# A diffusion layer from the output product on: weights as the moving operand, tokens standing, and the residual kept as rows

## The chip, the cores and the metric

The kernel runs on one core of a Trainium2 chip. The metric is the time of one execution on the device, in microseconds (us). The core has a matrix engine (PE, which multiplies a moving operand of up to 512 columns by a standing one of 128 x 128), a vector engine (DVE), a scalar engine (ACT), a general engine (POOL), and a queue that only issues transfers (SP). PE writes to PSUM, eight banks of 512 float32 columns; DVE and ACT read from it.

## The reference

One layer of a hybrid backbone on 1280 tokens of width 1024: 1024 latent tokens (eight blocks of 128) and 256 prompt tokens (two blocks), with a conditioning vector each.

```python
h = rms_norm(x, norm_mix_w) * (1.0 + sc1) + sh1
z = h @ w_in                        # recurrence q, f, f, i, g; attention q, k, v; gates gl
o_a = block_attention(q, k_all, v_all)
o_h = hgrn_branch(...)              # two directions, 4 heads, f = lb + (1 - lb) * sigmoid(hf), key = 1 - f
merged = g[:, :, 0] * (o_h @ w_ho) + g[:, :, 1] * (o_a @ w_ao)
x = x + g1 * (merged @ w_out)
h = rms_norm(x, norm_ffn_w) * (1.0 + sc2) + sh2
x = x + g2 * (jnp.square(jax.nn.relu(h @ w_ff1)) @ w_ff2)
y = rms_norm(x, final_norm_w)
```

All of it is float32. g1 and g2 are vectors of 1024 for each of the two conditions, latent and prompt.

## The kernel before

**Products.** Each float32 factor is split into a rounded high part (ACT, the first line of `split`) and the rest (DVE, its second line), and a product is three matmuls: high by high, high by rest, rest by high. Tokens come in three tiles `TT`: t=0 and t=1 with 512 latents each, t=2 with the 256 prompt tokens.

**Order of the work.** Projections and attention come first, then the recurrence, with the gate columns of w_in (and the conditioning product) filling PE between its small matmuls: a `Filler` deals them out in portions. Then come the branch products with the merge, the output product, the up-projection (w_ff1), and the down-projection (w_ff2). PE follows the order of the program. ACT, DVE, POOL and SP are ordered by a scheduler that simulates the program, with priority by program order; `tc.high_priority` moves an instruction ahead. From the up-projection on, SP too follows the order of the program. Each engine works strictly in its order.

**PSUM.** Three rings of banks: g (3), s (3) and t (2). Name p stands for g.

**Recurrence.** 24 units (`HUnit`: head, direction, tile). `prep` loads f and q, makes products of f along time by two scans on DVE, then k = 1 - f on ACT (in place of f), the scaled keys and queries on POOL and DVE. `keys_t` transposes keys to a bank of t, which ACT copies (`ukt`). `scores` makes scores in a bank of s, which DVE masks (`usm`); `states_` makes the states (s). `out`, one unit later, makes the outputs in a bank of g, which is copied on ACT (forward) or added to the forward output on DVE (`uo`, backward). The gate columns use banks of g.

**Output product.** The result has columns of w_out on partitions and tokens along the free axis: 128 x 128 pieces of w_out stand, the merged columns `mT` move (512 or 256 tokens). 48 groups (4 column pairs, 3 tiles, 2 halves), 24 matmuls each. `x_cols` loads x by columns (24 loads) and transposes it on PE; the group's sum is scaled by g1, which is a scalar for each partition here, and added in one DVE operation; `sq_acc` sums squares on ACT and DVE. `norm2_rstd` and `norm2` make the norm's factor by matmuls with a column of ones, spread it over partitions by matmuls with the identity, and apply it on DVE and ACT. `keep` stores the residual: latents as columns (`XA`), the prompt transposed to rows (`XT`).

**Up-projection.** The prompt's part is 32 groups of 24 matmuls of 256 columns. The latents' part uses Strassen's scheme with seven products: `sums1` builds the sums of activation blocks between the prompt's groups and `fsplit` splits them (`form`: B11 to T4). `fsums` does the same for weights.

**Down-projection.** Seven chains of 16 steps (`chain2`: P1, P2, P6, P7, P4, P5, P3) into five banks, 15 matmuls of 512 columns a step. For the latents (banks 0 to 3) weights `wh` stand and activations `ah` move; for the prompt's quarter (bank 4, `mm_p`) activations stand and weights move. `load_step` loads three steps ahead. `drain` adds finished banks to the residual, `gadd` in one DVE operation for latents, `pmul` and `padd` in two for the prompt. `sk` keeps P1's banks as a share of three other quarters, added later by `rest`. `final` transposes a block of latent columns to rows (8 transposes), and applies the last norm.

## Time and profile before

| | |
|---|---|
| runs | 2142.56, 2142.61, 2151.43 us; median 2142.61 |
| profiled execution | 2138.14 us; span 2136.4 us |
| mean granted PE clock | 0.993 |
| bytes moved | 316.64 MB in 251465 packets, mean 148 GB/s |

The profile shows one execution. Its page has busy times of the engines, and the groups of instructions with how long the engine stood idle before them and what ended that. "PE ps_g L302" is a matmul of line 302 into a bank of ring g, "A <- B" means that A waited until B was done. PEld is the loading of the standing operand, which goes on beside matmuls. Matmuls are pipelined: a record's duration is longer than the distance from one start to the next. In a table by windows a granted clock of 1.00 is full speed.

### The profile page before, as it was taken

The page shows a single profiled execution, that of the slowest core. Times are in us where ns is not written, and L with a number is a line of the kernel's source. Part 1 is how long each engine was busy: PE and PEld are TensorE (multiplying, and loading weights), DVE is VectorE, ACT ScalarE, POOL GpSimd, SP SyncE. Part 2 cuts the span into 40 slices and gives each one's busy share as a digit, 9 for nine tenths or more (in the row PEclk, how much of TensorE's full clock was granted, in tenths as well). Part 3 has the DMA queues.
Part 4 walks back from the last instruction along what each step waited for, and adds up shares of the span by engine and source line. Part 5 has one row for each costly group of instructions (what it writes and reads, how often), then busy time and mean ns, then how long its engine had stood idle before and what let it go on. Part 6 is the DMA issues. An engine that isn't in the chain of part 4 may idle for free.

```text
span 2136.4 us, 34621 instructions
## 1 busy us (share of the span) xinstructions
PE 2066.4 (97%) x12859; PEld 1779.6 (83%) x12859; DVE 1386.3 (65%) x2620; ACT 970.9 (45%) x2003; POOL 514.5 (24%) x545
## 2 busy tenths in 40 slices
PE   6899999999999999998999999999999999999998
PEld 4788889988899987887888888898888888888876
DVE  3784776676776888777353525966666665566684
ACT  4754555555555522222230425754555444333352
POOL 1372323332332445444112100222211110000010
PEclk9999999999999999999999999999999999999999
DMA  9365221241222255454634433674444488565763
GB/s 287 111 188 163 65 75 37 75 132 54 69 80 70 85 172 161 145 161 136 210 119 138 127 103 111 215 229 158 140 156 143 149 308 258 175 190 170 237 223 104
DMA packets 251465, 316.64 MB, mean 148 GB/s; under 512 B 18440, under 2 KB 171600, under 8 KB 251296
## 3 DMA queue, kind: packets, MB, share of 16 engines
q1 hardware_dynamic: 238912, 274.79, 40.8%
q0 software_dynamic: 12384, 39.64, 5.2%
q8 instruction: 101, 1.65, 0.3%
q14 instruction: 68, 0.56, 0.1%
HBM read 226.81 MB, written 87.56 MB: 147 GB/s over the span
## 4 chain that ended last, share of the span: by engine, by line
PE 48%; issue 29%; DVE 9%; DMA 7%; POOL 4%; ACT 3%; SPq 1%; POOLq 0%; DVEq 0%; ACTq 0%
PE ps_g L302 8%; PE ps_g L304 7%; PE ps_g L303 7%; PE ps_s L661 4%; PE ps_t L702 3%; POOL AF L102 3%; PE ps_g L718 2%; PE ps_g L717 2%; PE ps_g L318 2%; PE ps_g L320 2%; PE ps_g L319 2%; DMA wraw<-in_w_in 2%; PE ps_s L302 1%; PE ps_s L303 1%; PE ps_s L304 1%
## 5 line engine op out<-in xcount | busy, mean ns | idle before, releaser
L302 PE MATMUL ps_g<-hs,wsp 128*128 128x512 f32 (+1 forms) x960 | 357.8, 373 | 7.5 <-DVE uo L952 7.2
L304 PE MATMUL ps_g<-hs,wsp 128*128 128x512 f32 (+1 forms) x960 | 342.7, 357 | 0.0
L303 PE MATMUL ps_g<-hs,wsp 128*128 128x512 f32 (+1 forms) x960 | 342.1, 356 | 0.0
L680 POOL TENSOR_SCALAR pexp<-pexp,rs 128x512 f32<-128x512 f32 (+1 forms) x104 | 169.7, 1638 | 366.2 <-ACT pTh L705 184.2
L273 ACT ACTIVATE wsp<-wraw 128x1024 fp32r<-128x1024 f32 x118 | 117.9, 1000 | 260.8 <-PE ps_g L303 109.6
L274 DVE TENSOR_TENSOR wsp<-wraw,wsp 128x1024 fp32r<-128x1024 f32 x118 | 139.2, 1180 | 121.4 <-ACT wsp L273 121.0
L302 PEld LDWEIGHTS ps_g<-hs,wsp 128*128 128x128 f32 x960 | 182.3, 190 | 33.0 <-DVE uo L952 7.7
L304 PEld LDWEIGHTS ps_g<-hs,wsp 128*128 128x128 f32 x960 | 181.9, 190 | 27.3
L303 PEld LDWEIGHTS ps_g<-hs,wsp 128*128 128x128 f32 x960 | 182.7, 190 | 19.8
L705 ACT ACTIVATE pTh<-ps_t 128x512 fp32r<-128x512 f32 x200 | 118.9, 601 | 124.7 <-PE ps_t L702 122.2
L273 ACT ACTIVATE ah<-ar 128x640 fp32r<-128x640 f32 (+1 forms) x112 | 81.0, 723 | 199.1 <-PE ps_g L1479 185.6
L662 DVE TENSOR_REDUCE mx<-ps_s 128x1 f32<-128x512 f32 (+1 forms) x208 | 136.6, 662 | 51.3 <-PE ps_s L661 50.9
L672 ACT ACTIVATE pexp<-ps_s,ngm 128x512 f32<-128x512 f32 (+1 forms) x208 | 137.3, 669 | 43.1 <-DVE ngm L666 41.5
L706 DVE TENSOR_TENSOR pTl<-ps_t,pTh 128x512 fp32r<-128x512 f32 x200 | 135.8, 680 | 15.7 <-ACT pTh L705 15.2
L274 DVE TENSOR_TENSOR ah<-ar,ah 128x640 fp32r<-128x640 f32 (+1 forms) x112 | 89.8, 802 | 75.6 <-ACT ah L273 74.8
L661 PE MATMUL ps_s<-Kl,Ql 128*128 128x512 f32 (+1 forms) x416 | 128.0, 413 | 1.1 <-ACT pexp L672 1.1
L702 PE MATMUL ps_t<-ident,pexp 128*128 128x128 f32 x800 | 120.7, 273 | 3.0 <-DVE pTl L706 1.8
L318 PE MATMUL ps_g<-wsp,hs 128*128 128x256 f32 x400 | 117.4, 293 | 0.0
L319 PE MATMUL ps_g<-wsp,hs 128*128 128x256 f32 x400 | 114.0, 285 | 2.8 <-DVE wsp L274 2.8
L320 PE MATMUL ps_g<-wsp,hs 128*128 128x256 f32 x400 | 114.1, 285 | 0.0
L718 PE MATMUL ps_g<-pTl,Vl 128*128 128x256 f32 x400 | 106.1, 287 | 4.2 <-DVE pTl L706 4.1
L717 PE MATMUL ps_g<-pTh,Vl 128*128 128x256 f32 x400 | 105.9, 285 | 1.3 <-DVE oa L727 1.0
(389 smaller groups left out, 5368.0 us busy)
## 6 DMA issues: line engine op xcount, KB each, us to landing
ar<-AF SPq DMA_DIRECT2D x112, 320.0 KB, 3.2
wraw<-in_w_ff SPq DMA_DIRECT2D x32, 1024.0 KB, 6.0
wr<-in_w_ff SPq DMA_DIRECT2D x128, 256.0 KB, 3.7
wraw<-in_w_in SPq DMA_DIRECT2D x19, 1024.0 KB, 5.7
wraw<-in_w_ada SPq DMA_DIRECT2D x16, 1024.0 KB, 5.5
AF<-a POOLq DMA_DIRECT2D x48, 256.0 KB, 2.8
AF<-t POOLq DMA_DIRECT2D x48, 256.0 KB, 2.6
wa<-in_w_ada SPq DMA_DIRECT2D x32, 256.0 KB, 5.6
```

What stands on the lines that cost most here:

```text
L273: s_.activation(hi, raw, AF.Copy)
L274: v.tensor_tensor(lo, raw, f32(hi), op=ALU.subtract)
L302: pe.matmul(out, hi[:, k, :], mh, start=(first and k == 0), stop=False)
L303: pe.matmul(out, hi[:, k, :], ml, start=False, stop=False)
L304: pe.matmul(out, lo[:, k, :], mh, start=False, stop=(last and k == kcs - 1))
L318: pe.matmul(po[:, bb, :], mh[:, off:off + P], wh[:, k % 4, :], start=(k == 0), stop=False)
L319: pe.matmul(po[:, bb, :], mh[:, off:off + P], wl[:, k % 4, :], start=False, stop=False)
L320: pe.matmul(po[:, bb, :], ml[:, off:off + P], wh[:, k % 4, :], start=False, stop=(k == KC - 1))
L661: pe.matmul(pq[:, 0:n], self.qh[:, q0:q0 + P], K[self.g][var][self.kts[i]], start=(var == 0), stop=(var == 1))
L680: NORM[(i + j) % len(NORM)].tensor_scalar(x, x, self.rs[j], None, op0=ALU.mult)
L702: pe.transpose(pt[:, a, j * P:(j + 1) * P], self.Ps[j][i][:, b * P:(b + 1) * P], ident)
L718: pe.matmul(pv[:, 0:256], V[self.g][kg][:, b, :], lo[:, a, :], start=False, stop=(k == last))
```

## The change

- **Recurrence.** k = 1 - f goes to POOL. The outputs use ring s. The copies `ukt`, `usm` and `uo` get high priority.
- **Order of tiles** in the merge: t = 0, 2, 1.
- **Output product.** Tokens on partitions, columns along the free axis: a 128 x 128 piece of `mT` stands, 512 columns of w_out move; ten blocks of 128 tokens by two halves, 24 matmuls each. All of w_out is split into `WO` ahead, its first half during the merge, its second after it. x is loaded as rows. The gates, now along the free axis, are written as rows once (`gate_rows`) and read back spread over partitions; the add is two DVE operations (`out_add`). Squares are summed by ACT's accumulator; `out_norm` scales the row and stores the residual (`X1`); `norm2_t` transposes the normalised rows to columns.
- **Up-projection.** The transposes of t=1 run in groups 2 to 5 of the prompt's part. Two of the seven forms, B22 and T4, are split after it. Buffers are laid out anew (`H`, `slot`).
- **Down-projection.** All five banks use `mm_p`, activations standing. Drains are `gmul` and `radd`. The rings of the three sets of banks differ (`five`). `final` works on rows without transposes.

The diff, cut to its core:

```diff
+    def H(t, dt=F32R, name="hs"):
+        return hp.tile([P, 512] if t < 2 else [P, 2, 256], dt, tag="h%d" % t, name=name, bufs=16 if t < 2 else 8)
...
             k = self.k = f
-            s_.activation(k[:, 0:n], f[:, 0:n], AF.Identity, scale=-1.0, bias=1.0)
+            g_.tensor_scalar(k[:, 0:n], f[:, 0:n], -1.0, 1.0, op0=ALU.mult, op1=ALU.add)
...
             self.kts = S((P, 4, P), name="ukt")
-            s_.activation(self.kts[:, 0:self.nb], kt[:, 0:self.nb], AF.Copy)
+            with tc.high_priority(offset=400):
+                s_.activation(self.kts[:, 0:self.nb], kt[:, 0:self.nb], AF.Copy)
...
             self.sm = S((P, 4, P), name="usm")
-            v.tensor_tensor(self.sm[:, 0:nb], sc[:, 0:nb], masks[d].unsqueeze(1).broadcast_to([P, nb, P]), op=ALU.mult)
+            with tc.high_priority(offset=400):
+                v.tensor_tensor(self.sm[:, 0:nb], sc[:, 0:nb], masks[d].unsqueeze(1).broadcast_to([P, nb, P]), op=ALU.mult)
...
-            po = PS("p", (P, 4, P))
+            po = PS("s", (P, 4, P))
...
             o = self.o = S((P, 4, P), name="uo")
-            v.tensor_tensor(o[:, 0:nb], po[:, 0:nb], fwd.o[:, 0:nb], op=ALU.add)
+            with tc.high_priority(offset=400):
+                v.tensor_tensor(o[:, 0:nb], po[:, 0:nb], fwd.o[:, 0:nb], op=ALU.add)
...
     for cond in range(2):
         v.scalar_tensor_tensor(s2[:, cond], modc[:, cond, 32:40], 1.0, cols[:, NFFN:NFFN + 8], op0=ALU.add, op1=ALU.mult)
-        v.tensor_scalar(g1h[:, cond], modc[:, cond, 16:24], 0.5, None, op0=ALU.mult)
+        v.tensor_scalar(gc[:, 8 * cond:8 * cond + 8], modc[:, cond, 16:24], 0.5, None, op0=ALU.mult)
+        v.tensor_copy(out=gc[:, 16 + 8 * cond:24 + 8 * cond], in_=modc[:, cond, 40:48])
+    def gate_rows():
+        pt = PS("t")
+        pe.transpose(pt[0:32, 0:P], gc, ident)
+        e = S((32, P), name="gt0")
+        s_.activation(e, pt[0:32, 0:P], AF.Copy)
+        store(GR, e)
+    def gate_row(i, cond):
+        r = 16 * i + 8 * cond
+        return GR[r:r + 8, :].rearrange("(o a) b -> o (a b)", o=1).broadcast_to([P, D])
+    MT = (0, 2, 1)
-    for t, (t0, n, cond) in enumerate(TT):
+    for t in MT:
+        n = TT[t][1]
...
+    WO = [[None] * 4 for _ in range(2)]
+    def out_raw(half, kh):
+        r = wp.tile([P, 4, 512], F32, tag="wraw", name="wraw", bufs=2)
+        dma(r, I["w_out"][kh * 512:kh * 512 + 512, half * 512:half * 512 + 512].rearrange("(k p) c -> p k c", p=P))
+        return r
+    def out_w(half, kp, raw):
+        n = 2 * (4 * half + kp)
+        WO[half][kp] = hi, lo = [wsp((P, 2, 512)) if j < 4 else
+                                 (wo1 if j < 11 else wo2).tile([P, 2, 512], F32R, tag="wo%d" % j, name="wo") for j in (n, n + 1)]
+        split(hi, lo, raw)
     for c2 in range(4):
-        raws = []
...
             oc = 2 * c2 + half
             wh, wl = w_oc(r, half)
-            for t, (t0, n, cond) in enumerate(TT):
+            if oc == 1:
+                gate_rows()
+            for t in MT:
+                n = TT[t][1]
...
+        if c2 == 3:
+            for kp in range(4):
+                if kp % 2 == 0:
+                    raw = out_raw(0, kp // 2)
+                out_w(0, kp, raw[:, 2 * (kp % 2):2 * (kp % 2) + 2, :])
-    for t, (t0, n, cond) in enumerate(TT):
+    for t in MT:
...
+    xa = [[None] * KC for _ in range(2)]
+    h2 = [None] * KC
+    def new_cols(t):
+        if t == 0:
+            for t, kc in [(t, kb) for kb in range(4) for t in range(2)] + [(t, kb + 4) for t in (1, 0) for kb in range(4)]:
+                xa[t][kc] = H(0, F32, "xa")
+        elif t == 2:
+            for kc in range(0, KC, 2):
+                hi, lo = H(2), H(2)
+                h2[kc], h2[kc + 1] = [(hi[:, j], lo[:, j]) for j in range(2)]
+    xrow = {}
+    def load_row(b):
+        xrow[b] = xn.tile([P, D], F32, tag="x1", name="x1", bufs=6)
+        dma(xrow[b], xrows(b))
+    def load_g1b(t):
+        g = ob.tile([P, D], F32, tag="g1b", name="g1b", bufs=1)
+        dma(g, gate_row(0, TT[t][2]))
+        return g
+    def out_add(b, half, po, ss):
+        c = slice(half * 512, half * 512 + 512)
+        x, y = xrow[b][:, c], ob.tile([P, 512], F32, tag="y1", name="y1", bufs=2)
+        v.tensor_tensor(y, po, g1b[:, c], op=ALU.mult)
+        v.tensor_tensor(x, x, y, op=ALU.add)
+        s_.activation(y, x, AF.Square, accum_out=ss[:, half:half + 1])
+    def out_norm(b, ss):
+        dma(X1[b], xrow[b])
+        rst = T(4, "nrst")
+        v.tensor_tensor(ss[:, 2:3], ss[:, 0:1], ss[:, 1:2], op=ALU.add)
+        rstd_of(rst[:, 0:1], ss[:, 2:3], 1, 1.0 / D)
+        v.tensor_scalar(xrow[b], xrow[b], rst[:, 0:1], None, op0=ALU.mult)
+    def norm2_t(t, kc):
+        nb, cond = NB[t], TT[t][2]
+        pt = PS("t", (P, 4, P))
+        for j in range(4):
+            kj, b = (kc, j) if t < 2 else (kc + j // 2, j % 2)
+            pe.transpose(pt[:, j, :], xrow[4 * t + b][:, kj * P:(kj + 1) * P], ident)
+        if t < 2:
+            s_.activation(xa[t][kc], pt.rearrange("p b c -> p (b c)"), AF.Identity, scale=s2[:, cond, kc:kc + 1],
+                          bias=modc[:, cond, 24 + kc:25 + kc])
-            norm2_rstd(0)
+        hx = ob.tile([P, 4, P], F32, tag="y1", name="hx", bufs=2)
+        for j in range(2):
+            s_.activation(hx[:, 2 * j:2 * j + 2], pt[:, 2 * j:2 * j + 2], AF.Identity, scale=s2[:, cond, kc + j:kc + j + 1],
+                          bias=modc[:, cond, 24 + kc + j:25 + kc + j])
+        for j in range(2):
+            hi, lo = h2[kc + j]
+            split(hi, lo, hx[:, 2 * j:2 * j + 2].rearrange("p b c -> p (b c)"))
+    OB = (0, 1, 2, 3, 8, 9, 4, 5, 6, 7)
+    load_row(OB[0])
+    load_row(OB[1])
+    for kp in range(4):
+        if kp % 2 == 0:
+            raw = out_raw(1, kp // 2)
+        out_w(1, kp, raw[:, 2 * (kp % 2):2 * (kp % 2) + 2, :])
+    todo2 = []
+    for i, b in enumerate(OB):
+        t, off = b // 4, (b % 4) * P
+        if b in (0, 8, 4):
+            g1b = load_g1b(t)
+        ss = T(4, "oss2")
+        for half in range(2):
+            po = PSG()
+            for k in range(KC):
+                mh, ml = (x[:, off:off + P] for x in mT[t][k])
+                wh, wl = (x[:, k % 2, :] for x in WO[half][k // 2])
+                pe.matmul(po, mh, wh, start=(k == 0), stop=False)
+                pe.matmul(po, mh, wl, start=False, stop=False)
+                pe.matmul(po, ml, wh, start=False, stop=(k == KC - 1))
+                if half and todo2:
+                    todo2.pop(0)()
+            out_add(b, half, po, ss)
+            if half == 0 and i + 2 < len(OB):
+                load_row(OB[i + 2])
+        out_norm(b, ss)
+        if b in (3, 9):
+            new_cols(t)
+            todo2 = [lambda t=t, kc=kc: norm2_t(t, kc) for kc in range(0, KC, 1 if t == 0 else 2)]
...
...
+    def slot(f):
+        if f == "B22":
+            return H(2).rearrange("p a c -> p (a c)")
+        return H(1 if f in ("B21", "T1") else 0)
-        hi, lo = form[f][kb]
-        if lo is None:
-            lo = form[f][kb][1] = xp.tile([P, 512], F32R, tag="xa", name="form", bufs=18)
-        split(hi, lo, src)
+        hl = form[f][kb]
+        for i in range(2):
+            if hl[i] is None:
+                hl[i] = slot(f)
+        split(*hl, src)
...
+            fsplit("B21", kb, b21)
             t1 = t1s[kb] = pw.tile([P, 512], F32, tag="t1", name="t1", bufs=2)
             v.tensor_tensor(t1, b12, b11, op=ALU.subtract)
-            fsplit("T1", kb, t1)
             fsplit("B11", kb, b11)
         elif part == 1:
-            t3 = pw.tile([P, 512], F32, tag="t1", name="t3", bufs=2)
+            t3 = t3s[kb] = pw.tile([P, 512], F32, tag="t1", name="t3", bufs=2)
             v.tensor_tensor(t3, b22, b12, op=ALU.subtract)
             v.tensor_tensor(b12, b22, t1s[kb], op=ALU.subtract)
-            fsplit("B21", kb, b21)
-            fsplit("T3", kb, t3)
+            fsplit("T1", kb, t1s[kb])
         else:
             v.tensor_tensor(b21, b21, b12, op=ALU.subtract)
-            fsplit("B22", kb, b22)
+            fsplit("T3", kb, t3s[kb])
             fsplit("T2", kb, b12)
-            fsplit("T4", kb, b21)
     for i in range(NP):
...
             wt = w_oc(r, half)
-            mid = {3: lambda: norm2_rstd(1), 4: lambda: norm2(1)}.get(j)
+            mid = (lambda: (norm2_t(1, 2 * j - 4), norm2_t(1, 2 * j - 3))) if 2 <= j < 6 else None
             po = PSG()
             mm3(po[:, 0:256], wt, KC, h2, mid=mid)
...
     w_next = fsums(raw1(0))
-    close("pw", "h2p")
+    close("pw", "xn")
+    for kb in range(4):
+        fsplit("B22", kb, xa[1][kb + 4])
+    for kb in range(4):
+        fsplit("T4", kb, xa[0][kb + 4])
...
-        return ev.tile([P, 512], F32, tag="ev", name=name, bufs=14)
+        return ev.tile([P, 512], F32, tag="ev", name=name, bufs=13)
...
+        if 20 <= n < 36 and n % 2 == 0:
+            load_x1(row_loads.pop(0))
         if n == 54:
             load_fw()
         if n in (12, 14):
-            dma(xt[n // 2 - 6], XT[n // 2 - 6])
+            load_x1(8 + n // 2 - 6)
+        if n in (16, 18):
+            dma(g2b[n // 2 - 8], gate_row(1, n // 2 - 8))
...
-            more = dict(skip_group_check=not first)
-            for m in range(4):
+            for m in range(4 if name == "P3" else 5):
                 c = slice(m * P, (m + 1) * P)
-                pe.matmul(banks[m], wh[:, c], ah[:, 0:512], start=first and i == 0, stop=False, **more)
-                pe.matmul(banks[m], wh[:, c], al[:, 0:512], start=False, stop=False, **more)
-                pe.matmul(banks[m], wl[:, c], ah[:, 0:512], start=False, stop=i == NP - 1, **more)
-            if name != "P3":
-                mm_p(banks[4], i, (ah[:, 512:640], al[:, 512:640]), (wh, wl), first, False)
+                mm_p(banks[m], i, (ah[:, c], al[:, c]), (wh, wl), first)
+    xt = [None] * 10
+    def load_x1(b):
+        xt[b] = xo.tile([P, D], F32, tag="x1", name="x1", bufs=10)
+        dma(xt[b], X1[b])
...
+    def gmul(half, m, src):
+        y = cs("y")
+        v.tensor_tensor(y, src, g2b[m // 4][:, half * 512:half * 512 + 512], op=ALU.mult)
         return y
-    def padd(b, i, y):
-        c = slice(i * 512, (i + 1) * 512)
-        v.tensor_tensor(xt[b][:, c], xt[b][:, c], y, op=ALU.add)
-    def drain(t, half, banks, b):
+    def radd(t, half, m, y):
+        x = xt[blk(t, m)][:, half * 512:half * 512 + 512]
+        v.tensor_tensor(x, x, y, op=ALU.add)
+    def drain(t, half, banks):
         with tc.high_priority(offset=400):
-            for m in range(4):
-                gadd(t, 4 * half + m, banks[m])
-            y = pmul(half, banks[4])
-        padd(b, half, y)
+            for m, po in enumerate(banks):
+                radd(t, half, m, gmul(half, m, po))
...
+    def final(b, put=store):
+        ss, rst = ssf[b], T(4, "frst")
+            x = xt[b][:, c]
+            v.scalar_tensor_tensor(x, x, rst[:, 0:1], fw[:, c], op0=ALU.mult, op1=ALU.mult)
+            put(out_rows(b)[:, c], x)
...
+    X = five("gggss")
     chain2("P1", X, True)
-    chain2("P2", X, False, {2: make_g2b})
-    drain(0, 0, X, 0)
-    Y = five()
+    chain2("P2", X, False)
+    drain(0, 0, X)
+    Y = five("ttsgg")
     chain2("P6", Y, True)
-    drain(1, 0, Y, 1)
-    rest = [lambda t=t, h=h, m=m: gadd(t, 4 * h + m, sk[m]) for t, h in ((0, 1), (1, 0), (1, 1)) for m in range(4)]
-    rest += [lambda b=b, h=h: padd(b, h, pmul(h, sk[4])) for b, h in ((0, 1), (1, 0), (1, 1))]
+    drain(1, 0, Y)
+    yk = {}
+    def share(m, j):
+        if j == 0:
+            yk[m] = gmul(1, m, sk[m])
+            radd(0, 1, m, yk[m])
+        elif j == 1:
+            radd(1, 1, m, yk[m])
+        else:
+            radd(1, 0, m, gmul(0, m, sk[m]))
+    rest = [lambda m=m, j=j: share(m, j) for m in range(5) for j in range(3)]
     chain2("P7", Y, False, dict(enumerate(rest[0:8], 4)))
-    drain(1, 1, Y, 1)
+    drain(1, 1, Y)
     chain2("P4", Y, False, dict(enumerate(rest[8:], 4)))
-    drain(0, 1, Y, 0)
-    Z = five()
-    at = {3 * b + 2: lambda b=b: final(0, b) for b in range(4)}
+    drain(0, 1, Y)
+    Z = five("gsstt")
+    at = {}
+    for j, b in enumerate((0, 1, 2, 3, 8)):
+        at[3 * j + 1] = lambda b=b: (square(b, 0), square(b, 1))
+        at[3 * j + 2] = lambda b=b: final(b)
     chain2("P5", Z, True, at)
-    drain(1, 1, Z, 1)
-    at = {3: lambda: square_p(0, 0), 4: lambda: square_p(0, 1), 6: lambda: final_p(0), 8: lambda: square_p(1, 1)}
-    chain2("P3", Z, False, at)
+    drain(1, 1, Z)
+    chain2("P3", Z, False, {2 * j + 4: lambda b=b: square(b, 1) for j, b in enumerate((4, 5, 6, 7, 9))})
     for m in range(4):
-        gadd(1, m, Z[m])
+        radd(1, 0, m, gmul(0, m, Z[m]))
+        square(4 + m, 0)
+    for m in range(4):
+        final(4 + m, dma)
     for i in range(NP):
-        mm_p(Z[4], i, p3f[i], p3w[i], False, True)
-        if i in (3, 6, 9, 12):
-            final(1, i // 3 - 1, "ts"[i // 3 % 2] * 2, dma)
-    padd(1, 0, pmul(0, Z[4]))
-    square_p(1, 0)
-    final_p(1, dma)
+        mm_p(Z[4], i, p3f[i], p3w[i], False)
+    radd(1, 0, 4, gmul(0, 4, Z[4]))
+    square(9, 0)
+    final(9, dma)
```

215 lines of the change are left out of this document (46 added, 169 removed).

## The prediction

> **What bounds the kernel now.** The page's first lines come first, then a table of the stages by windows of time.
>
> ```profile
> span 2136.4 us, 34621 instructions
> PE 2066.4 (97%) x12859; PEld 1779.6 (83%) x12859; DVE 1386.3 (65%) x2620; ACT 970.9 (45%) x2003; POOL 514.5 (24%) x545
> ```
>
> PE is busy for 97% of the span: a change pays if it takes matmuls away or ends one of PE's few stops, and work taken from another engine alone is worth nothing. The profiled execution took 2138.1 us, 1.7 more than its span and 4.5 less than the median of 2142.6; I sum against 2138.1 and add 4.5 at the end. The stages that the change touches are the recurrence, output product, up-projection (prompt part, then the latents' seven products), down-projection and end. The columns are the stretch, its length, then busy time and instructions of PE, weight loads, DVE, ACT and POOL, the granted clock, and DMA:
>
> ```profile
> 720.00:1040.00 320.00, 303.28 (x2504) 258.44 (x2503) 244.02 (x585) 97.91 (x260) 140.96 (x154) 0.97 0.47 149
> 1200.00:1322.00 122.00, 119.80 (x672) 103.15 (x670) 46.60 (x81) 37.61 (x70) 2.09 (x2) 1.00 0.33 108
> 1322.00:1424.00 102.00, 97.37 (x797) 95.20 (x796) 88.70 (x141) 77.59 (x142) 23.32 (x30) 1.00 0.72 223
> 1424.00:1735.00 311.00, 310.98 (x1351) 252.91 (x1349) 198.01 (x274) 152.98 (x228) 62.09 (x114) 1.00 0.46 155
> 1735.00:2112.00 377.00, 374.85 (x1663) 307.86 (x1664) 248.74 (x389) 150.66 (x265) 10.43 (x17) 1.00 0.66 213
> 2112.00:2136.40 24.40, 15.26 (x83) 12.43 (x81) 11.11 (x24) 5.79 (x18) 2.72 (x5) 0.88 0.28 108
> ```
>
> The recurrence is the one stage with much to win: PE stands for 320 - 303.3 = 16.7 us there, and it alone of the first five rows has a clock under 1.00. The up-projection's prompt part loses 4.6 us. The view of waits says for whom PE stood:
>
> ```profile
> PE ps_g L302 <- DVE uo L952: 7.2, 2, 4.9
> PE ps_s L921 <- ACT ukt L902: 3.2, 3, 1.4
> PE ps_t L900 <- DVE usf L871: 1.7, 1, 1.7
> PE ps_g L940 <- ACT ze L1011: 1.2, 1, 1.2
> PE ps_s L304 <- DVE wsp L274: 2.6, 4, 1.0
> PE ps_g L304 <- DVE wsp L274: 1.7, 1, 1.7
> PE ps_t L1119 <- ACT xte L1176: 1.5, 1, 1.5
> PE ps_t L1174 <- ACT xte L1176: 0.7, 1, 0.7
> ```
>
> The first four are the recurrence's, the next two the prompt part's, and the last two fall where the prompt's residual is turned to rows for keeping. The longest, 7.2 us, is a gate matmul that has no free bank of ring g because an output of the recurrence still lies in one, waiting for its add on DVE.
>
> **The change part by part: small matmuls.** What disappears on PE are transposes and one-column or broadcast matmuls: the final rows' (L1543), the kept prompt rows' (L1174), the second norm's sums and broadcasts (L1139, L1148) and the prompt gate's (L1565). A mean duration overlaps its neighbours, so I price by starts:
>
> ```profile
> L1543 PE MATMUL ps_t<-ident,xa 128*128 128x128 f32 x48 | 6.2, 272 | 0.0
> L1543 PE MATMUL ps_s<-ident,xa 128*128 128x128 f32 x16 | 2.1, 272 | 0.0
> L1148 PE MATMUL ps_t<-ident,nrst 128*128 128x128 f32 x20 | 2.8, 280 | 0.0
> L1139 PE MATMUL ps_t<-ones,qacc 128*128 128x1 f32 x20 | 2.4, 238 | 0.0
> L1174 PE MATMUL ps_t<-ident,xa 128*128 128x128 f32 x16 | 2.4, 281 | 0.7 <-ACT xte L1176 0.7
> L1565 PE MATMUL ps_t<-ident,modc 128*128 128x128 f32 x16 | 1.9, 275 | 0.0
> 2115.15 1.03 PE L1543 MATMUL ps_s<-ident,xa 128*128 128x128 f32 x8
> 2115.94 0.48 PE L1478 MATMUL ps_g<-p3w,p3f 128*128 128x512 f32 x1
> 2116.26 0.40 PE L1479 MATMUL ps_g<-p3w,p3f 128*128 128x512 f32 x1
> 1249.51 0.28 PE L302 MATMUL ps_g<-hs,wsp 128*128 128x256 f32 x1
> 1249.98 0.28 PE L303 MATMUL ps_g<-hs,wsp 128*128 128x256 f32 x1
> ```
>
> Eight transposes take 2115.94 - 2115.15 = 0.79 us, and the matmul behind them 0.32 us where its like takes 0.23 (311 us over 1351 in the latents' stretch), so 0.88 for eight, 0.11 each. The six rows count 48 + 16 + 20 + 20 + 16 + 16 = 136, which is **-15.0 us**, all on PE's path. The 80 transposes that bring x to columns (10 blocks by 8 pieces) stay 80: the new second norm needs as many, later. One is added, for the gate rows: 0.1.
>
> **The products.** The prompt's 192 matmuls of 256 columns in the output product become 96 of 512. Four of the narrow take 0.47 us (1249.98 - 1249.51), so 192 take 22.6 and 96 wide ones at 0.23 take 22.1: **-0.5**. In the down-projection each step keeps 15 matmuls of 512 columns; exchanging what stands costs nothing, because the prompt's columns already run with tokens standing:
>
> ```profile
> L1508 PE MATMUL ps_g<-ah,wh 128*128 128x512 f32 x192 | 75.2, 392 | 0.0
> L1478 PE MATMUL ps_g<-wh,ah 128*128 128x512 f32 x96 | 37.5, 391 | 0.2 <-DVE yp L1570 0.2
> ```
>
> **Stops in the middle.** Nothing is turned to rows for keeping, so the two waits for xte go: **-2.2**. In the prompt part DVE is busy for 88.7 of 102 us and loses the latents' second-norm scalings and eight form splits, 16 operations on whole tiles. Of its 4.3 us of waits for weight splits I take half, **-2.2**, between nothing and all.
>
> **The recurrence.** Its outputs leave ring g for ring s, and the copies that free banks go ahead in DVE's and ACT's order. What stands behind a stop is its clock; the same view in short stretches:
>
> ```profile
> 834.00:836.80 2.80, 0.57 (x24) 0.30 (x12) 2.08 (x6) 0.00 (x0) 1.11 (x1) 1.00 0.32 117
> 836.80:840.30 3.50, 3.43 (x35) 2.21 (x35) 2.65 (x8) 1.45 (x6) 0.81 (x2) 0.51 0.34 72
> 888.00:891.50 3.50, 2.07 (x13) 1.74 (x13) 2.38 (x5) 1.94 (x8) 1.55 (x2) 0.99 0.45 152
> 891.50:895.00 3.50, 3.50 (x12) 2.69 (x11) 3.50 (x6) 2.10 (x6) 1.53 (x1) 0.52 0.11 43
> 986.00:989.50 3.50, 3.50 (x8) 2.77 (x9) 2.77 (x10) 1.93 (x8) 0.81 (x2) 0.50 0.59 188
> ```
>
> After each stop PE runs about 3.5 us at half clock, which loses 1.75. The two stops for uo (7.2) lie before the first and third such stretch: with them go 3.5, together **-10.7**, which I take whole, because a gate tile then finds a third bank. The stops for ukt and ze (4.4) and the half clock at 891.5 (1.75) are ACT's; they are left out, since ACT's new order is nowhere shown: the range has them, 6.1 more. *TensorE: Matmul & The Clock Gate* of the Trainium skill (Part 1) says that the clock falls after an idle window of about 3.4 us; by that only the 4.9 us stop would return clock, and my time would be 1.75 us higher. The rows here decide otherwise: the clock fell behind a stretch in which PE still worked 2.07 of 3.5 us.
>
> Moving 1 - f to POOL frees ACT, which stands in order behind it, but puts a longer instruction on the way to the keys:
>
> ```profile
> L847 ACT ACTIVATE uf<-uf 128x512 f32<-128x512 f32 (+1 forms) x24 | 13.4, 560 | 76.1 <-DVE usf L844 40.5 <-DVE usf L840 28.8 <-DVE usf L839 3.8
> L680 POOL TENSOR_SCALAR pexp<-pexp,rs 128x512 f32<-128x512 f32 (+1 forms) x104 | 169.7, 1638 | 366.2 <-ACT pTh L705 184.2
> L871 DVE TENSOR_TENSOR uw<-uq,um x24: 410/896/1508, 743.5 to 1024.7; 128x512 f32<-128x512 f32 x16, 128x256 f32<-128x256 f32 x8
> L274 DVE TENSOR_TENSOR wsp<-wraw,wsp 128x1024 fp32r<-128x1024 f32 x118 | 139.2, 1180 | 121.4 <-ACT wsp L273 121.0
> 2127.84 0.68 DVE L1570 TENSOR_TENSOR yp<-ps_g,g2b 128x512 f32<-128x512 f32 x1
> 2129.09 0.68 DVE L1576 TENSOR_TENSOR xt<-xt,yp 128x512 f32<-128x512 f32 x1
> ```
>
> 1.64 for 0.56 is 1.08 us more per unit. POOL has 141 us of work in 320, so it is hidden but at the first unit, where PE already waited 1.7 us for usf: **+1.1**. Behind it on POOL wait the unit's own key product, the scaled queries and the score add of the unit before.
>
> **What is added.** (1) The second half of w_out is split only when the merged tiles leave room: at worst eight merged splits of 0.68 and four weight splits of 1.18 follow one another, 10.2 us, where PE asks for the first after 24 x 0.23 = 5.5: a stop of 4.7, with clock 6.4; at best all is early. I take **+1.0**, near the low end, because DVE is busy for only 46.6 of 122 us there. (2) A drain is now two DVE operations a bank (0.68 + 0.68) where PE fills a bank in 0.69. Three drains are followed by a product into the same banks: the fifth bank is read 5 x 1.36 - 0.68 = 6.1 us after the first is full, PE wants it after 8 x 0.69 = 5.5: 0.6 each, **+1.8**; nothing if the scheduler reads all banks first, 8.4 if a step's splits (2.2) stand ahead each time. The 15 shares skipped between are covered by 377 - 249 us of idle DVE. (3) At the end four blocks want 16 DVE operations while PE does 48 matmuls (11 us): 16 x 0.68 is 10.9, as long as PE's part, with three short steps for each block between, so **+1.0**, between 0 and 2. (4) Eight splits of B22 and T4 move into the first latent pair; DVE has 113 idle us in that stretch, cost 0; without that cover 8 x 0.68 = 5.4. (5) DMAs: 24 column loads, 20 stores and 18 loads of the residual become 10 + 10 + 10 of rows, with one gate store on POOL's queue and five broadcasts on SP's; w_out stays four loads. SP is not PE's releaser in any row above, cost 0; a row load ahead of the next step's activations is covered by three steps of lead, 10 us.
>
> Sum: -15.0 - 0.5 - 2.2 - 2.2 - 10.7 + 0.1 + 1.1 + 1.0 + 1.8 + 1.0 = -25.6. On 2138.1 this is 2112.5, and with 4.5 to the median **2117 us**.
>
> **The rivals.** *The recurrence gives nothing*: DVE, busy for 244 of 320 us, is late for the next user of the bank instead. For it speaks DVE's load, against it that the stops name one ring. 2117 + 10.7 = 2128. *Both that and the upper ends of (1) to (3)*: 5.4 + 6.6 + 1 more, 2141. *The recurrence becomes slower*: POOL's longer operation comes onto PE's path at each of 24 units, 24 x 1.08 = 26 us, and if each stop halves the clock once, 42 more: 2154 to 2196, say 2175. It decides once a unit's preparation has less than 1.1 us of slack. Against it: PE waited for a preparation once, and POOL would have 7 of a unit's 13.3 us. For it: DVE's scaled queries range from 410 to 1508 ns, so something beside them slows them. The GPSIMD Engine Reference of the Trainium skill (section 1, Specifications) says that POOL's way to SBUF is shared with DVE's two-input operations; by it, 24 more POOL operations stretch DVE too.
>
> **How the numbers follow.** Forecast 0.62 (2103 to 2127), first rival 0.19, second 0.12, third 0.07. The low end is 2117 less 6.1 (ACT's stops), 2.1 (the prompt part's other half) and 4.8 (nothing added); the high end takes in the first rival with half the second's extra, 2136. About 0.5%, 10.7 us, is what a measurement of this kernel can tell from no change: under 2131.9 lie the forecast and nearly all of the first rival, 0.80; within lies the second, 0.13; slower the third, 0.07.
>
> **What would show it.** Right: no L1543 and no xte rows; PE's records about 230 fewer (136 and 96); no wait of a gate matmul for uo, and clock 1.00 through most of 720 to 1040; no stop over 1 us in the first 10 us of the output product; the down-projection as long as before less some 5 us of transposes; stops under 1 us behind the three drains. Wrong: PE waiting for usf, uw or a score in many units (third rival), or for wo at the output product's start.

## The result, and the profile after

The changed kernel takes 2120.65 us (median of four runs, 2118.32 to 2121.50) against 2142.59: ratio 0.989 (95% interval 0.9874 to 0.9906), 21.9 us less. The profiled execution took 2121.06. The forecast was 2117, within 2103 to 2136.

First the page's head, then the stages by windows of time: the recurrence, the output product, the prompt part, the latents' seven products, the down-projection, and the end. Columns as in the table of before.

```profile
span 2119.3 us, 34118 instructions
PE 2047.2 (97%) x12628; PEld 1764.3 (83%) x12628; DVE 1405.8 (66%) x2651; ACT 954.4 (45%) x1971; POOL 541.6 (26%) x577
757.00:1038.00 281.00, 274.95 (x2298) 233.42 (x2298) 218.81 (x501) 72.04 (x194) 141.08 (x163) 0.99 0.51 162
1189.00:1310.00 121.00, 116.24 (x527) 95.28 (x526) 52.24 (x92) 34.47 (x75) 7.66 (x10) 0.99 0.34 118
1310.00:1408.50 98.50, 96.84 (x806) 96.44 (x805) 73.24 (x117) 67.97 (x123) 22.48 (x30) 1.00 0.73 229
1408.50:1718.60 310.10, 306.39 (x1346) 253.32 (x1346) 200.44 (x278) 155.19 (x232) 59.96 (x110) 0.99 0.44 147
1718.60:2099.80 381.20, 375.15 (x1635) 307.36 (x1634) 266.15 (x421) 156.78 (x276) 16.81 (x20) 1.00 0.67 221
2099.80:2119.30 19.50, 11.31 (x49) 8.79 (x47) 12.56 (x28) 3.13 (x10) 2.76 (x5) 0.88 0.36 134
```

PE has 231 records fewer. The recurrence's half-clock stretches are nearly gone, but in the output product, the seven products and the down-projection PE now stands for 4.8, 3.7 and 6.0 us (length less busy time), where before it was 2.2, 0 and 2.1. The view of waits names the stops, and windows of 3.5 us show the clock behind three of them:

```profile
PE ps_s L927 <- ACT ukt L907: 4.0, 4, 1.8
PE ps_g L1388 <- ACT s L1399: 3.7, 1, 3.7
PE ps_g L1527 <- DVE y L1586: 2.8, 1, 2.8
PE ps_g L1528 <- DVE ah L278: 2.7, 2, 2.3
PE ps_t L1197 <- DVE x L1189: 2.2, 2, 1.2
PE ps_g L1229 <- DVE wo L278: 2.2, 1, 2.2
PE ps_g L308 <- DVE wsp L278: 1.7, 1, 1.7
PE ps_t L904 <- DVE usf L875: 1.6, 1, 1.6
1199.80:1203.30 3.50, 3.50 (x10) 2.80 (x9) 1.76 (x3) 0.00 (x0) 0.00 (x0) 0.53 1.01 388
1418.40:1421.90 3.50, 3.50 (x10) 2.72 (x10) 1.71 (x5) 0.00 (x0) 0.77 (x1) 0.51 0.22 67
1892.80:1896.30 3.50, 3.50 (x10) 2.68 (x9) 3.50 (x6) 1.26 (x2) 0.00 (x0) 0.51 0.01 5
```

No gate matmul waits for uo, and xte is gone; the waits for ukt and usf are what is left in the recurrence, and that for wsp what is left of 4.3 us in the prompt part. In their place stand five stops at seams that the change made: for wo (the output product's second half of weights), x (the second norm's rows), s (the first bank of the seven products, behind the splits that were moved there), ah (the down-projection's third step) and y (the drain from chain P6 to P7).

One profile is not enough for sizes of a few us: attention and all before it, which the two kernels issue in the same order on PE, DVE and ACT (but for a few small operations on the gates), ended 4.7 us later here. So I measured the stages in the traces of all the kernels below, from the first matmul of one to the first of the next (the recurrence up to its last output matmul, the end from the last matmul on). Each row is one execution:

| kernel | start to attention | recurrence | output product, prompt part | seven products | six chains | P3, four banks | fifth bank | end |
|---|---|---|---|---|---|---|---|---|
| before | 752.8 | 291.0 | 226.2 | 309.7 | 335.1 | 46.2 | 14.5 | 9.5 |
| b_rec | 756.6 | 282.1 | 227.2 | 309.6 | 338.6 | 46.0 | 14.5 | 9.6 |
| b_ring | 753.7 | 282.4 | 227.7 | 309.6 | 335.5 | 46.1 | 14.5 | 9.5 |
| b_prio | 753.1 | 291.4 | 227.3 | 309.5 | 338.9 | 45.7 | 14.5 | 9.5 |
| b_pool | 756.4 | 291.2 | 226.2 | 309.6 | 337.5 | 47.1 | 14.5 | 9.6 |
| b_pad | 754.0 | 292.2 | 226.2 | 307.5 | 337.8 | 46.4 | 14.4 | 9.6 |
| after | 757.5 | 280.5 | 219.2 | 310.2 | 335.8 | 45.2 | 11.0 | 8.6 |
| a_pad | 755.8 | 281.9 | 219.9 | 309.8 | 335.8 | 44.3 | 10.8 | 8.7 |
| a_phase | 757.9 | 282.6 | 220.0 | 315.2 | 337.1 | 45.7 | 11.0 | 8.6 |
| a_halves | 753.3 | 282.0 | 215.6 | 310.9 | 335.9 | 46.0 | 11.0 | 8.6 |
| a_s1 | 754.7 | 282.9 | 218.7 | 306.9 | 337.6 | 44.9 | 11.0 | 8.6 |
| a_drain | 757.0 | 281.4 | 217.2 | 311.2 | 337.3 | 45.3 | 11.0 | 8.6 |
| a_all | 753.5 | 282.0 | 214.9 | 306.1 | 337.0 | 43.5 | 10.8 | 8.6 |
| a_all2 | 753.2 | 282.3 | 216.4 | 306.9 | 333.1 | 43.9 | 10.8 | 8.6 |

(The merge takes 151.3 to 151.5 in all.) The first column varies by 5 us whatever the kernel: those 4.7 us are chance. Names with b_ are edits of the kernel before, names with a_ of the changed one.

### The profile page after: what moved, and what is told of

It is laid out like the page before. It is cut to its first block, busy times and chain, and to the rows that moved or that the text cites. A ratio compares the mean times of both kernels' runs of the same rounds, so it can differ in the third digit from the quotient of the medians.

```text
span 2119.3 us, 34118 instructions
## 1 busy us (share of the span) xinstructions
PE 2047.2 (97%) x12628; PEld 1764.3 (83%) x12628; DVE 1405.8 (66%) x2651; ACT 954.4 (45%) x1971; POOL 541.6 (26%) x577
## 4 chain that ended last, share of the span: by engine, by line
PE 46%; DVE 2%; DMA 2%; issue 2%; ACT 1%; POOL 0%; SPq 0%; DVEq 0%; POOLq 0%; ACTq 0%
PE ps_g L306 2%; PE ps_g L308 2%; PE ps_g L307 2%; PE ps_g L1529 2%; PE ps_g L1527 2%; PE ps_g L1528 2%; PE ps_s L1390 2%; PE ps_s L1389 2%; PE ps_s L1388 2%; PE ps_s L1527 2%; PE ps_s L1528 2%; PE ps_s L1529 2%; PE ps_g L1388 1%; PE ps_g L1390 1%; PE ps_g L1389 1%
## 5 line engine op out<-in xcount | busy, mean ns | idle before, releaser
L306 PE MATMUL ps_g<-hs,wsp 128*128 128x512 f32 (+1 forms) x896 | 323.2, 361 | 0.0
L308 PE MATMUL ps_g<-hs,wsp 128*128 128x512 f32 (+1 forms) x896 | 310.5, 347 | 1.7 <-DVE wsp L278 1.7
L307 PE MATMUL ps_g<-hs,wsp 128*128 128x512 f32 (+1 forms) x896 | 309.8, 346 | 0.0
L277 ACT ACTIVATE wsp<-wraw 128x1024 fp32r<-128x1024 f32 x112 | 111.5, 997 | 262.2 <-PE ps_g L307 78.9
L308 PEld LDWEIGHTS ps_g<-hs,wsp 128*128 128x128 f32 x896 | 169.9, 190 | 23.8 <-DVE wsp L278 1.9
L306 PEld LDWEIGHTS ps_g<-hs,wsp 128*128 128x128 f32 x896 | 170.2, 190 | 20.4 <-issue 5.0
L307 PEld LDWEIGHTS ps_g<-hs,wsp 128*128 128x128 f32 x896 | 170.6, 190 | 15.5
```

Of the source, the lines that this page charges most:

```text
L277: s_.activation(hi, raw, AF.Copy)
L306: pe.matmul(out, hi[:, k, :], mh, start=(first and k == 0), stop=False)
L307: pe.matmul(out, hi[:, k, :], ml, start=False, stop=False)
L308: pe.matmul(out, lo[:, k, :], mh, start=False, stop=(last and k == kcs - 1))
```

## The experiments

**The recurrence.** Three edits came together; all three, then each alone.

```
b_rec   all of the recurrence's hunks of the diff
b_ring  - po = PS("p", (P, 4, P))        + po = PS("s", (P, 4, P))
b_prio  + with tc.high_priority(offset=400):   around the copies ukt, usm, uo
b_pool  - s_.activation(k, f, AF.Identity, scale=-1.0, bias=1.0)
        + g_.tensor_scalar(k, f, -1.0, 1.0, op0=ALU.mult, op1=ALU.add)
```

> The kernel before with the recurrence's edits alone: 1 - f on POOL, the outputs in ring s, and the three copies that free banks put ahead in DVE's and ACT's order. From the recurrence's first transpose to its last output the stage took 291.1 us before and 280.4 after. Theory A (the edits themselves made it 10.7 shorter, whatever stands around them): the stage takes 279 to 282, no gate matmul waits for uo, and the whole is 9 to 12 us shorter than before, about 2132. Theory B (the stage became shorter through the other places of the tiles or through chance): 289 to 292, the whole within 2 us of before. Attention, which both kernels issue in the same order on PE, DVE and ACT, ended at 748.7 us before and 753.4 after: if that is chance, this kernel's attention ends anywhere between the two; if it is the tiles' places, it ends at 748 to 750.

Measured: 2136.73 against 2142.95, ratio 0.9966 (0.9953 to 0.9979). Theory A on the stage: 282.1 against 291.0. The whole is 6.2 us shorter by the medians, less than the 9 to 12 that A gave.

> The kernel before with one word changed: the recurrence's outputs take their bank in ring s instead of ring g. Theory A1 (the gate matmuls waited because an output held one of ring g's three banks): the 7.2 us of waits for uo go, and with them the two half-clock stretches behind them, 7 to 11 us, so about 2133 to 2136. Theory A2 (they waited because DVE came late to the output; the order of DVE is what counts): a score or state matmul of ring s waits for uo in their place, and the time stays within 3 us of before.

Measured: 2135.69, ratio 0.9966 (0.9952 to 0.9981), stage 282.4. Waits, of this kernel:

```profile
PE ps_s L921 <- ACT ukt L902: 6.3, 4, 3.0
PE ps_t L900 <- DVE usf L871: 1.8, 1, 1.8
```

A1: the waits for uo are gone with one word, and nothing in ring s waits for uo instead. Part of the gain is lost to the waits for ukt, 3.2 us before and 6.3 here (3.6 with all three edits, at the same stage time).

> The kernel before with one edit: the three operations that free a bank of the recurrence (the key transposes' copy, the masked scores, the output's add) are put ahead in DVE's and ACT's order. Theory A1 (the ring decides): the waits for uo stay, 5 us or more of the 7.2, and the time is within 3 us of before. Theory A2 (DVE's order decides): they fall under 2 us and the time is 7 to 11 us shorter.

Measured: 2143.91, ratio 1.0001 (0.9986 to 1.0015), stage 291.4.

```profile
PE ps_g L302 <- DVE uo L955: 7.1, 2, 4.8
```

But the edit left the order as it was: of DVE's 519 operations between 740 and 1045 us only two masks (usm) change places, of ACT's 226 none. At the longest stop PE stands from 981.0 before and 981.4 here, and in both the add comes 4 us later, behind the same weight split. Before, then here:

```profile
984.31 1.23 DVE L274 TENSOR_TENSOR wsp<-wraw,wsp 128x1024 fp32r<-128x1024 f32 x1 [0.33 <-ACT wsp L273]
985.45 0.42 DVE L952 TENSOR_TENSOR uo<-ps_g,uo 128x256 f32<-128x256 f32 x1
```

```profile
984.54 1.22 DVE L274 TENSOR_TENSOR wsp<-wraw,wsp 128x1024 fp32r<-128x1024 f32 x1 [0.19 <-ACT wsp L273]
985.69 0.41 DVE L955 TENSOR_TENSOR uo<-ps_g,uo 128x256 f32<-128x256 f32 x1
```

So A2 is not tested by this run: an add that really came first might have ended the stop as well.

> The kernel before with one edit: 1 - f is done on POOL instead of ACT in all 24 units. My prediction had it cost 1.1 us once, in the first unit, and nothing else. Rival C1 (ACT, freed of 24 x 0.56 = 13.4 us, is no longer late with ukt and ze): the 4.4 us of waits for them and the 1.75 of clock behind one of them go, 3 to 6 us shorter. Rival C2 (POOL's 1.64 for ACT's 0.56 comes onto PE's path): up to 26 us longer.

Measured: 2144.13, ratio 1.0003 (0.9992 to 1.0014), stage 291.2.

```profile
PE ps_g L302 <- DVE uo L952: 9.1, 2, 6.0
PE ps_t L900 <- DVE usf L871: 2.3, 1, 2.3
PE ps_t L900 <- DVE um L862: 1.0, 1, 1.0
```

The ring alone is enough for the whole saving. The priorities, which hardly moved an operation, leave 7.1 us of waits where they were. 1 - f on POOL lengthens the first unit's waits from 1.7 to 3.3 us, as forecast in kind. The waits for ukt and ze fall from 4.4 to 2.0, as C1 said, but those for uo grow from 7.2 to 9.1, and the stage stays as long as it was: neither C1 nor C2 in the time.

**Where tiles lie.** The seven products gave no stop to explain a difference of pace: in a stretch of 50 us without stops, PE issues 218 matmuls before and 222 after. In the last products it is slow in both (155 and 156 in 36 us, where 0.227 us apart would be 159). The columns are those of the windows, before first:

```profile
1471.00:1521.00 50.00, 50.00 (x218) 40.71 (x217) 32.52 (x45) 26.37 (x38) 9.04 (x18) 1.00 0.45 147
2072.00:2108.00 36.00, 36.00 (x155) 28.93 (x155) 23.92 (x45) 14.78 (x31) 1.99 (x3) 1.00 0.50 162
```

after:

```profile
1458.00:1508.00 50.00, 50.00 (x222) 41.41 (x221) 30.31 (x43) 24.79 (x37) 9.17 (x17) 1.00 0.47 153
2060.00:2096.00 36.00, 36.00 (x156) 28.91 (x155) 23.81 (x44) 16.70 (x36) 0.00 (x0) 1.00 0.47 148
```

```
b_pad, a_pad  + ctx.enter_context(tc.tile_pool(name="pad", bufs=1, side="right")).tile([P, 8], F32, ...)
                xb = pool("xb", "right")
a_phase         F1 = pool("F1")
              + F1.tile([P, 16], F32, tag="pad", name="pad")
```

> The kernel before with a tile of 32 bytes per partition put ahead of everything on the right-hand side of the on-chip memory and never used: every tile on that side moves by 32 bytes. In before, 895 of 5760 matmuls with 512 columns read an operand whose address is 32 over a multiple of 64 bytes; here none does. In the latents' seven products the trace of before has starts 230.5 ns apart on average where the low part of a form lies so (256 of 1344), and in the down-projection's last 240 products of stationary tiles 233 to 234; after, whose 1344 all lie on multiples of 64, has 226.7 in the first, and in its last products, whose moving tiles lie 32 off, again 233. Theory D (the address decides): the seven products take 305 to 306.5 instead of 309.8 us, the last part (P3's first four banks) 44 to 45 instead of 46.2, attention up to 2.7 less (384 such matmuls at 7 ns), the whole 5 to 8 us shorter, about 2136. Theory E (the place in memory, its neighbours or the traffic decide, not the 32 bytes): all stages within 0.5 us of before.

Measured: 2137.03, ratio 0.9976 (0.9965 to 0.9987). The seven products take 307.5, half of what D said, and the last products do not move. The rest of the 5.7 us is in no stage that the table could name: the profiled execution is, with 2141.08, one of the two slowest of its twelve. Windows:

```profile
1474.00:1524.00 50.00, 50.00 (x221) 41.14 (x220) 33.19 (x45) 26.94 (x39) 9.59 (x18) 1.00 0.45 150
2075.00:2111.00 36.00, 36.00 (x156) 29.02 (x155) 23.59 (x45) 14.91 (x31) 2.00 (x3) 1.00 0.50 160
```

> The changed kernel with the same unused tile of 32 bytes per partition ahead of everything on the right-hand side. There 624 of 5856 matmuls with 512 columns read an operand 32 over a multiple of 64 bytes (384 scores of attention, 240 in the down-projection's last products); here none does. Theory D (the address decides): the last products' first four banks take 43.5 to 44 us instead of 45.2, the fifth bank's 48 matmuls 0.3 less, attention up to 2.7 less: 1.5 to 4.6 us shorter than after. Theory E: within 0.5 us in these stages.

Measured: 2120.16, ratio to before 0.989 (0.9871 to 0.9908). Here the last products do speed up, while the starts of attention's scores stay 232.0 ns apart (234.3 in after):

```profile
2060.00:2096.00 36.00, 36.00 (x161) 29.80 (x160) 24.19 (x45) 16.68 (x36) 0.00 (x0) 1.00 0.47 148
```

So 32 bytes decide something, but "a multiple of 64" is not the rule. Sorting the matmuls of five traces by the places of both operands gave another: the moving tile and the next standing one begin at the same place within 512 bytes, or they do not.

> The changed kernel with 64 unused bytes per partition ahead of the pool that holds 17 of the 56 form tiles, and nothing else. The padded versions showed that 32 bytes are not the whole rule: of the seven products' matmuls in before with the pad those whose form lies 448 over a multiple of 512 bytes, with weights 64 over one, still start 234 ns apart and the others 227, while in after with the pad the last products, moving and stationary tiles both 448 over, have 226.7. Theory N (moving and stationary tile must begin at the same place within 512 bytes): 28 of a pair's 84 products (all of the first, 7 of the second, 9 of the fifth) take 234 ns, so the stage is 3.2 us longer than in after. Theory D (a multiple of 64 bytes is enough): 226.7 throughout, the stage within 0.5 us of after.

Measured: 2126.43, the stage 315.2 against 310.2. The stretch of 50 us holds 220 matmuls. The fourth and the seventh product keep 227 ns at every position; the first, second and fifth, and the starts of the third and sixth right behind them, have 226 to 241. Stops left out, the mean goes from 226.7 to 229.6 ns, which over 1343 is 3.9 us, a little more than N's 3.2; the rest is a longer clock stretch. N holds, D falls. Only differences of 32, 64, 320, 352, 384 and 416 bytes occurred.

```profile
1462.00:1512.00 50.00, 50.00 (x220) 40.88 (x219) 30.54 (x42) 23.09 (x34) 9.17 (x17) 1.00 0.48 158
```

**The new stops.** Each of these edits is worth about as much as the uncertainty of a whole time (some 3.5 us either way), and none of the three whole times differs clearly from after's 2120.65. They are judged by the stage and its stops, in one trace each.

```
a_halves  output product's order: (block 0, half 0), (1, 0), (0, 1), (1, 1), then as before
a_s1      T4's high parts:  s_.activation -> g_.tensor_copy
a_drain   drain P6 to P7, m > 2:  y = new("wr"); s_.activation(y, po, AF.Copy); y times g2b on DVE
```

> The changed kernel with one edit: in the output product PE does the first half of the columns for the first two blocks of tokens before the second half of either, so that the second half of w_out is asked for 24 matmuls (5.5 us) later. In after PE waits 2.2 us for its low part at 1196 and a half-clock stretch of 3.4 us follows. Theory J (the split is late by about 2.5 us and no more): no wait there, 3.5 to 4 us shorter than after. Rival K (each split waits for its tile's place, which the merge's last tiles hold, and then for its neighbours): the stop stays, smaller, and 0 to 2 us are gained.

Measured: 2118.87; the stage 215.6 against 217.2 to 220.0 in the five others with the old order, and no wait for wo is left. Theory J on the stage; the whole is 1.8 us shorter.

> The changed kernel with one edit: in the latents' first pair the rounded high parts of the four T4 forms are made by POOL instead of ACT. In after ACT stands 2.3 and 0.9 us in front of two of them, because each needs a tile that DVE frees with a B22 split, and behind them stands the copy of the first bank, for which PE waits 3.7 us at 1414; a half-clock stretch follows. Theory H (ACT's order behind these two waits is the whole of it): the stop and the clock loss go, 5 to 5.5 us shorter than after. Rival I (DVE, with 16 split parts, sums and weight splits in that pair, is late next): PE waits for T4 or for a weight split 10 us later, and at most 3 us are gained.

Measured: 2120.70; the stage 306.9, 3.3 less. The wait for s is gone, and none for T4 or a weight split came; but a shorter one, which neither theory named, did: the fifth product (S3 x T3) wants the bank that DVE still has to read into u2.

```profile
PE ps_s L1390 <- DVE u L1404: 2.0, 1, 2.0
```

> The changed kernel with one edit: at the drain between the third and the fourth chain of the down-projection (P6 to P7) the last two banks are copied out by ACT, and DVE multiplies by the gate from that copy. In after PE waits there 2.8 us for a bank that DVE reads after four splits and sums of the next steps, and a half-clock stretch of 3.4 us follows. Theory F (DVE's order at the drain is the whole of it): the stop and the clock loss go, 4 to 5 us shorter than after. Rival G (the splits that stood ahead of the read are late next): PE waits for ah or wh one step further, and 0 to 2 us are gained.

Measured: 2121.00; the six chains 337.3 against 335.8. Rival G: the stop for y is gone and one of 2.1 us for a weight split stands three steps on. That the chains are longer is not the edit's doing: in this trace the stop for ah too was followed by a half-clock stretch, which in after it was not.

```profile
PE ps_t L1529 <- DVE wh L278: 2.1, 1, 2.1
```

**Together.**

> The changed kernel with four edits together: 32 unused bytes ahead on the right-hand side, T4's high parts by POOL, the last two banks of one drain copied by ACT, and the output product's first halves first. If each edit takes away its own stop and nothing stands behind it, the sum is 1.9 to 4.6 + 5.4 + 4.5 + 3.9, 15.7 to 18.4 us shorter than after, 2102 to 2105. If what stands behind the stops is late next (rivals G, I and K), 3 to 8 us shorter, 2113 to 2118.

Measured: 2111.40, ratio to before 0.9846 (0.9831 to 0.9861): 9 us less than after, between the two forecasts.

```
a_all2  - if f == "B22": return H(2)       + if f == "T4": return H(2)     (T4 split first, then B22, high parts on POOL)
        - chain2("P7", Y, False, dict(enumerate(rest[0:8], 4)))      + chain2("P7", Y, False)
        - chain2("P6", Y, True)            + chain2("P6", Y, True, dict(enumerate(rest[0:8], 4)))
```

> The changed kernel with five edits, two of them new. Kept: 32 unused bytes ahead on the right-hand side, the output product's first halves first, and the high parts of the last four forms of the first pair by POOL. New (1): B22 and T4 exchange their tiles and their turn. In after the down-projection's third step waits 2.6 to 3.1 us for ah, because its loads are queued on SP behind two weight loads that wait 11.4 us for the place of T4, which the very last of the seven products reads; with B22 there, read one product (2.7 us) earlier, the wait should shrink to 0 to 0.5. If SP's queue itself or the loads' landing is the cause, it stays. New (2), instead of ACT's copies, which only moved the stop three steps on: eight of the residual's shares are added one chain earlier, so that at the drain between P6 and P7 five instead of three of the eight scratch tiles are free. Theory L (DVE reads the fourth bank late because its scratch tile waits for the first add): the 2.9 us stop falls under 0.5 and none comes behind it. Theory M (DVE has too much to do there): a stop of 2 us stays within the next four steps. All true: 2104 to 2107; only the first three: 2111.

Measured: 2107.22 (2105.35 to 2108.47), ratio to before 0.9829 (0.9807 to 0.9851), the lowest here, though its interval overlaps that of a_all. New (2) is right: theory L, 0.3 us is left at the drain and nothing comes behind it. New (1) fell: SP's wait for the tile went from 11.4 to 8.0 us, and ACT had the third step's high part at 1714.2, 4.4 us before PE asked in vain for the rest, but the stop stayed.

```profile
PE ps_g L1536 <- DVE ah L279: 3.1, 2, 2.8
1714.96 0.69 DVE L1477 TENSOR_TENSOR wS<-wr 128x512 f32<-128x512 f32 x1
1719.88 0.69 DVE L1489 TENSOR_TENSOR s2c<-wS,a11c 128x512 f32<-128x512 f32 x1 [4.24 <-issue]
```

DVE stood 4.24 us in front of the first weight sum, s2c, with ah's split queued behind it. It did the same in after (first fence), and not in before (second), where the same pair of instructions follow at once:

```profile
1723.56 0.69 DVE L1469 TENSOR_TENSOR wS<-wr 128x512 f32<-128x512 f32 x1
1728.51 0.69 DVE L1481 TENSOR_TENSOR s2c<-wS,a11c 128x512 f32<-128x512 f32 x1 [4.27 <-issue]
```

```profile
1735.80 0.68 DVE L1422 TENSOR_TENSOR wS<-wr 128x512 f32<-128x512 f32 x1
1736.52 0.69 DVE L1434 TENSOR_TENSOR s2c<-wS,a11c 128x512 f32<-128x512 f32 x1
```

By the programs' addresses the first s2c tile lies after the change on the tile of t3 of the last pair, which a store on POOL's queue still reads, and before on that of s1, last read by DVE itself. The change renumbers these tiles (FREED2). The times of landing point to this store: in after it lands at 1728.43 and s2c starts at 1728.51, in a_all2 at 1719.81 and 1719.88, and in all eight traces of the changed kernel and its edits s2c starts 0.08 us after it. A kernel with another number was not run.

## Why the prediction was right, and where not

The mechanism and its largest terms were right; 2117 was 3.6 us short. Most of the signs named beforehand came true: no xte and no final transposes, 231 records fewer, no gate matmul waiting for uo, and the clock. Two did not: the stop for wo 7 us into the output product, which was named as a sign of being wrong, and the 2.8 us behind a drain. By the table, with means over the kernels that share a stage's code:

- **Small matmuls**, -15.0. The fifth bank's part is 14.5 to 11.0, 3.5 for 32 transposes; in the chains of before four groups of eight cost 0.80 each and the sixteen of the prompt gate 1.7. That is 0.10 to 0.11 each, as priced. The output product's 56 lie among other differences there.
- **The recurrence**, -10.7 + 1.1. 291.5 (four kernels with the output in ring g) to 282.0 (ten with it in s): -9.4. The ring is enough for it; the high priorities, which I put beside it, moved next to nothing. POOL's 1.1 shows in the first unit's waits and not in the stage, and the third rival never came up.
- **Output product and prompt part**, -10.1 in this stage: 226.8 (six) to 219.0 (five): -7.8. Half the wsp waits were to go; 4.3 became 1.7, a little more. Step (1) was mis-sized: +1.0 was written, the stop and its clock cost 4.0 in after (a_halves gives 3.4 back against the mean; in a_s1 and a_drain the same stop cost no clock). The waits for x (2.2) and hx (0.3) were not in the sum. By these corrections the stage should have come out about 2 us longer than it did; where these lie no run shows. (The product had 24 groups before, 4 by 3 by 2, not 48.)
- **Step (4)**, eight splits at no cost because DVE has 113 idle us in the stretch. It failed: the stop of 3.7 and the half clock cost 5.3 (3.3 that a_s1 gives back, and the 2.0 of its own new stop). The stage's idle time lay elsewhere; in this pair DVE is busy from 1404.8 to 1420.1 without a gap, and ACT stood in order behind DVE with the copy that frees the bank. What made the stage only 0.9 longer (309.6 to 310.5) was a gain nobody forecast, the pace of its matmuls. That is luck: without it the time would have been some 4 us longer, 2125, still within the range.
- **Step (2)**, three stops of 0.6. It was one of 2.8, with 1.75 of clock behind it in after (in a_pad and a_phase without), and the other two are near nothing. The number of operations was right and the buffer was missed: the products need scratch tiles, of which five of eight were held (a_all2).
- **Step (5)**, DMAs at no cost. The third step's 2.3 us wait and the small ones around it cost 3.4 more than the same place did before. I looked at queues and not at which tile a buffer is laid over.
- **The six chains** came out 0.8 shorter (337.2 to 336.4) for these reasons, where the sum had about 4. Of the second rival's extra about half of the upper ends of (1) and (2) came true and nothing of (3); of the first rival nothing.
- **Step (3)**, +1.0 at the end: -0.9. DVE is through with the four blocks at 2111.1, as PE ends its last 48 matmuls (2110.7).
- The base: the profiled execution of before had the shortest start of fourteen (752.8), so the 4.5 to the median was right to add.

## What to carry to other kernels

Here a stop for a bank went with one word, the bank's ring. A priority is a request: after such an edit look whether the order changed, or its run tests nothing. A change of layout makes new seams: at each, ask which tile the first loads, sums and scratch lie on, and what reads that place last. Idle time summed over a stage says nothing of its first microseconds.

## What the runs showed of the hardware

**Pace by place.** A float32 matmul of 512 columns starts 227 ns after the last where the moving tile and the next standing one begin at the same place within 512 bytes (226.7 to 227.7 by trace and stage; some 11,700 from the seven products on in before, b_pad, after, a_pad and a_phase, those next to a slow one left out), and 229 to 234 where they do not (some 1,950): 233.2 in after's last products, 226.7 with 32 unused bytes ahead. With 256 columns there was no such difference: attention's 800 products have moving tiles at the same place before and 352 bytes off after, and starts 119.0 and 119.7 ns apart (gaps over 180 ns left out). *SBUF — State Buffer* of the Trainium skill ("SBUF: two separate sides") says that PE never waits on another reader of the memory, and in the table of its part on bandwidth pools that weights have a read port of their own; these runs cannot say whether PE's two reads meet in one bank, but by them the two are not independent of where the data lie.

**The clock.** Stops of 2.1 (a_drain), 2.2, 2.8 and 3.7 us (after) were each followed by about 3.4 us at half clock; one of 2.3 (after, at 1727) and those of 2.0 in a_s1 and 1.9 in a_all2 were not; and the stop of 2.8 for y, followed by one in after, a_halves and a_s1, was not in a_pad and a_phase. The clock's own records explain it. Within each of the fourteen traces the half-clock stretches lie on one grid of 3.41 us, and each is one or more whole windows of it (but the last, which the end cuts off). Between 130 and 2085 us, no full-clock window in which PE stood for less than 1.43 us was followed by one at half clock, and every one with more than 1.78 us was; 65 were, of some 7,900. So about half a window of standing still is enough, and a stop across a window's edge can be longer without loss: that for y in a_pad has 1.64 us in one window and the rest in the next. *TensorE: Matmul & The Clock Gate* of the Trainium skill (Part 1) has the clock fall after an idle window of about 3.4 us that runs freely. That it runs freely agrees with these traces; that it must be idle throughout does not.
